# A hybrid encoder layer on one core: attention and memory heads advance on a new step plan, with other counts of convolution taps

## The chip, the cores and the metric

The kernel runs on one core of a Trainium2 chip. The metric is the device time of one execution in microseconds. Five engines work side by side: TensorE (PE in the profile) multiplies, VectorE (DVE), ScalarE (ACT) and GpSimd (POOL) do elementwise work, SyncE (SP) issues DMAs. ScalarE and GpSimd issue DMAs as well.

## The reference, cut to what matters

One layer of a streaming encoder over 512 prompt frames and 64 sample frames (576 tokens, 2048 channels), all in float32.

```
mk, mv = split(mem_prompt @ w_mem_kv)            # 256 memory tokens
ca, cb, cg, q, k, v, ag, mq, mg = split(x @ w_in)
u = ca * sigmoid(cb)                             # conv branch, 1024 channels
y = layer_norm(causal depthwise conv(u, width 31) + conv_b)
conv = silu(y) @ w_pw
att = chunked attention(q, k, v, relative bias)  # 4 heads x 128, own chunk and 8 before it
mem = softmax(mq @ mk^T / sqrt(128)) @ mv        # 4 heads x 128
mix = concat(conv * silu(cg), att * silu(ag), mem * silu(mg))
out = layer_norm(ALPHA * x + mix @ w_out)
```

The outputs are `out` for both groups, the keys and values, the memory keys and values, and the last 30 convolution rows.

## The kernel before

Every float32 operand of a large matmul is split in two parts, `hi` (a cast by ScalarE) and `lo` (the rest, by VectorE), and the product is three matmuls: hi·hi, lo·hi, hi·lo. Weights come as 128x1024 blocks by DMA on SP's queue (`w_load`, line 165), five or more stages ahead, and are split two stages ahead (`w_split`, line 189). A *stage* is what TensorE does with one block.

The stages follow each other in this order on TensorE: the value projection (to about 60 us), 16 column pairs of the input projection by a seven-product scheme (`strassen`, to about 420 us; eight conv pairs, then eight gate pairs), four attention heads (`self_block`: k and q, two stages of 48 matmuls each), the memory projection (`mem_kv`, 16 steps of 18 matmuls), four memory heads (`mem_block`, two stages each), the second half of the output projection (the *out stage* below: 4 column groups n of 4 stages with 28 matmuls), the pointwise convolution product (`tileA(srhs, 1)`), the first half of the output projection, and the closing norm.

Work beside the stages is queued. `pump` (line 210) is called after each stage. It advances the generators in the queue `side` by `steps`, then runs `ntaps` closures of the queue `taps`. A tap is one VectorE instruction of the depthwise convolution over 128x606; each of the eight channel blocks has 31: `first` (which fetches the spilled input `up`), 29 middle ones, and `last`, which makes `y` and spills it. That is 248 in all. The counts are set by `TAP_RATE` (attention), `TAP_RATE_KV` (every second step of `mem_kv`), `TAP_RATE_MEM`, `TAP_RATE_OUT` and `TAPS_OF_PRODUCT` (seven products of a pair).

The generators are `self_attn` (line 692), `mem_attn` (line 588) and `conv_ln` (line 878). Each `yield` ends a step. `self_attn` has seven steps: load bias and cache; scores, maximum, exponential; scaling; transposes of the first two tiles (`pt`, lines 752 to 762); transposes of the rest (lines 771, 775); product with V; gating (`gated`, line 664). A head's generator is queued when its q is done and so runs under the next block's stages; the last head's runs under `mem_kv`, whose six accumulators hold six of the eight PSUM banks. `mem_attn` has five: loads; scores, softmax and scaling; transposes; product; gating. `conv_ln` is queued by the last tap. It takes the mean (one matmul over the sum of the `y`), squares, `var` (line 903), the diagonal `dg` (line 912), the matmuls `ra` that spread it (line 917), eight multiplications and eight SiLUs (lines 923, 924). The eight results are then split to `sx` (lines 1021, 1022) for the pointwise product. `late_mix` pumps until the mix tiles of the coming stage exist, and splits them.

The program is written with a tile framework. It gives every instruction a priority by its place in the program, plans each engine's queue when the program is built, with its own estimates, and lets a later instruction pass where an earlier one's operands or buffers are not expected yet. Tiles of one tag share a fixed number of buffers (`t5` 24, `t6` 11, weights 14, PSUM banks 8).

Of the kernel before, what the change touches and what calls it, by code (L numbers as in the profile page):

```python
# [9 lines left out]
F32 = mybir.dt.float32  # L10
# [5 lines left out]
P = 128  # L16
# [5 lines left out]
H = 4  # L22
# [13 lines left out]
HS = NS_TOK // 2  # L36

C_CA, C_CB, C_CG, C_Q, C_K, C_V, C_AG, C_MQ, C_MG = (0, 1024, 2048, 3072, 3584, 4096, 4608, 5120, 5632)
TAP_RATE = 2
TAP_RATE_KV = 1  # L40
TAP_RATE_MEM = 1
TAP_RATE_OUT = 6
TAPS_OF_PRODUCT = (2, 1, 1, 2, 1, 1, 2)
WARM = 8
CONV_PAIRS = [(C_CA + j * P, C_CB + j * P) for j in range(NCB)]
GATE_PAIRS = [(c + j * P, c + (j + 1) * P) for c, n in ((C_CG, NCB), (C_AG, H), (C_MG, H)) for j in range(0, n, 2)]
# [64 lines left out]
def hymba_kernel(ctx: ExitStack, tc: tile.TileContext, wst, xT, memT, xp, xs, kcT, vc, mkcT, mvc, biasx,  # L111
# [92 lines left out]
                w_load(j)  # L204
        return whi[i], wlo[i]

    side = deque()
    taps = deque()

    def pump(ntaps=0, steps=1):  # L210
        while side and steps:
            try:
                next(side[0])
                steps -= 1
            except StopIteration:
                side.popleft()
        for _ in range(ntaps):
            if not taps:
                break
            taps.popleft()()  # L220

    def drain():
        while side:
            pump()

    sidx = [0]
# [3 lines left out]
        sidx[0] += 1  # L230
        return weights(i)

    def tileA(rhs, nstage, ntaps=0, steps=1):
        accs = [bank("accA") for _ in range(2)]
        klist = list(range(8, 16)) + list(range(8)) if nstage == 2 else list(range(8))
        for s in range(nstage):
            hi, lo = next_stage()
            for kk in range(8):
                ki = 8 * s + kk
                k = klist[ki]  # L240
                ws = slice(kk * P, (kk + 1) * P)
                xh, xl = rhs(k)
                for pi, (mv, stat) in enumerate(((xh, hi), (xl, hi), (xh, lo))):
                    for c, acc in enumerate(accs):
                        nc.tensor.matmul(acc[:, :HALF], stat[:, ws], mv[:, c], start=ki == 0 and pi == 0,  # L245
                                         stop=ki == len(klist) - 1 and pi == 2)
            pump(ntaps, steps)
        return accs

    def tileB(lhs, tiles, sample, klist, ntaps=0, before=None, early=False, steps=1):  # L250
        accs = [bank("accB") for _ in tiles]
        sacc = bank("accS") if sample else None
        nk = len(klist)
        for s in range(nk // 2):
            if before:
                before(s)
            hi, lo = next_stage()
            for kk in range(2):
                ki = 2 * s + kk
                k = klist[ki]  # L260
                ws = slice(kk * 512, (kk + 1) * 512)
                st, en = ki == 0, ki == nk - 1
                if early and st:
                    for t, acc in zip(tiles, accs):
                        nc.tensor.matmul(acc, lhs(k, t)[0], hi[:, ws], start=True, stop=False)
                    for t, acc in zip(tiles, accs):
                        nc.tensor.matmul(acc, lhs(k, t)[0], lo[:, ws], start=False, stop=False)
                    for t, acc in zip(tiles, accs):
                        nc.tensor.matmul(acc, lhs(k, t)[1], hi[:, ws], start=False, stop=False)
                else:  # L270
                    for t, acc in zip(tiles, accs):
                        lh, ll = lhs(k, t)
                        nc.tensor.matmul(acc, lh, hi[:, ws], start=st, stop=False)  # L273
                        nc.tensor.matmul(acc, ll, hi[:, ws], start=False, stop=False)  # L274
                        nc.tensor.matmul(acc, lh, lo[:, ws], start=False, stop=en)  # L275
                if sample:
                    ss = sample(k)
                    nc.tensor.matmul(sacc, ss, hi[:, ws], start=st, stop=False)  # L278
                    nc.tensor.matmul(sacc, ss, lo[:, ws], start=False, stop=en)  # L279
            pump(ntaps, steps)  # L280
        return accs, sacc
# [138 lines left out]
    ysb = [None] * NCB  # L420
    ups = {}
    spilled = set()
    ln_left = [True]
    y_dram = [dram([P, NT], "yd") for _ in range(NCB)]
    s1 = [None]

    def queue_conv(j):
        acc = []
        up = [None]

        def fetch(j):
            ups[j] = t6([P, UPW], "up")
            nc.sync.dma_start(ups[j], up_dram[j])

        def first():
            for i in (j, j + 1):
                if i in spilled and i not in ups:
                    fetch(i)
            up[0] = ups[j]
            a = spool.tile([P, ACCW], F32, tag="t6", bufs=N6, name=nm("acc"))  # L440
            acc.append(a)
            nc.vector.tensor_scalar(a, up[0][:, :ACCW], cw_sb[:, j, 0:1], cp_sb[:, 0, j:j + 1], op0=ALU.mult, op1=ALU.add)

        def tap(t):
            def f():
                nc.vector.scalar_tensor_tensor(acc[0], up[0][:, t:t + ACCW], cw_sb[:, j, t:t + 1], acc[0],  # L446
                                               op0=ALU.mult, op1=ALU.add)
            return f

        def last():  # L450
            t = TAPS - 1
            y = t6([P, NT], "y")
            o = NP_TOK + 30
            for w, o, ys in ((HP, 0, slice(0, HP)), (HS, o, slice(HP, HALF))):
                yv = y.rearrange("p (a b) -> p a b", a=2)[:, :, ys]
                uv, av = (m.rearrange("p (a b) -> p a b", a=2)
                          for m in (up[0][:, o + t:o + t + 2 * w], acc[0][:, o:o + 2 * w]))
                nc.vector.scalar_tensor_tensor(yv, uv, cw_sb[:, j, t:t + 1], av, op0=ALU.mult, op1=ALU.add)
            nc.gpsimd.dma_start(y_dram[j], y)
            if j == 0:  # L460
                s1[0] = y
            elif j == 1:
                y0, s1[0] = s1[0], t6([P, NT], "s1")
                nc.vector.tensor_add(s1[0], y0, y)
            else:
                nc.vector.tensor_add(s1[0], s1[0], y)
            if j == NCB - 1:
                side.append(conv_ln())

        taps.append(first)  # L470
        for t in range(1, TAPS - 1):
            taps.append(tap(t))
        taps.append(last)
# [14 lines left out]
    def conv_sink(j):  # L488
# [5 lines left out]
        def both(c1, sg):  # L494
# [4 lines left out]
            nc.vector.tensor_mul(up[:, 572:636].rearrange("p (a b) -> p a b", a=2), c1[:, :, HP:], sg[:, :, HP:])  # L499
            nc.scalar.copy(cs_sb[:, j, :30], up[:, 512:542])  # L500
            nc.scalar.copy(cs_sb[:, j, 30:], up[:, 606:636])
            nc.gpsimd.dma_start(up_dram[j], up)
            spilled.add(j)
            queue_conv(j)
        return second, both
# [83 lines left out]
    def mem_attn(h, qh, ql, qs):  # L589
# [38 lines left out]
            nc.scalar.activation(pv, pv, AF.Copy, scale=sm[:, t:t + 1])  # L628
        nc.scalar.activation(pss[:64], pss[:64], AF.Copy, scale=sm[:64, 4:5])
        yield  # L630
        pT = []
        for b in range(2):
            tb = bank("mpt")
# [10 lines left out]
            nc.tensor.transpose(tb[:, b * 64:(b + 1) * 64], pss[:64, b * P:(b + 1) * P], ident[:64, :64])  # L644
        sT = t5([P, P], "msT")
        nc.vector.tensor_copy(sT, tb[:, :P])
        yield
        ob = bank("mo")
        os_ = bank("mos")
# [41 lines left out]
    def self_attn(h, qh, ql, qs, kh, kl, k):  # L691
# [54 lines left out]
            nc.scalar.activation(pt[:, po:po + w], pt[:, po:po + w], AF.Copy, scale=sm[:, t:t + 1])  # L746
        nc.scalar.activation(pS[:64, :576], pS[:64, :576], AF.Copy, scale=sm[:64, 4:5])
        yield
        b0 = bank("pt0")
        for t in range(4):  # L750
            pt, po = pplace[t]
# [46 lines left out]
        gated(mix, ob, os_, gate)  # L798
        mixraw[8 + h] = mix

    def self_block(h):
        k = evac2(tileA(xrhs, 2, TAP_RATE, 2), "k")
        nc.gpsimd.dma_start(kT_out[:, h], k.rearrange("p a b -> p (a b)"))
        kh = t5([P, 512], "kh", F32R)
        kl = t5([P, 512], "kl", F32R)
        khv, klv = (m.rearrange("p (a b) -> p a b", a=2) for m in (kh, kl))
        nc.scalar.copy(khv, k[:, :, :HP])
        nc.vector.tensor_sub(klv, k[:, :, :HP], khv.bitcast(F32))
        qh, ql, qs = evac_q(tileA(xrhs, 2, TAP_RATE, 2))
        side.append(self_attn(h, qh, ql, qs, kh, kl, k))  # L810


    mraw = {}
    mv_sb, mk_sb = [], []

    def load_mem(k):
        raw = t5([P, NMEM], "mraw")
        nc.sync.dma_start(raw, memT[:, k])
        mraw[k] = raw

    def mem_kv():
        for k in range(3):
            load_mem(k)
        mkacc = [bank("mkacc") for _ in range(H)]
        mvacc = [bank("mvacc") for _ in range(2)]
        for k in range(KD):
# [38 lines left out]
            mv_sb.append((mvh, mvl))  # L865

    def mem_block(h):
        qh, ql, qs = evac_q(tileA(xrhs, 2, TAP_RATE_MEM, 3))
        side.append(mem_attn(h, qh, ql, qs))


    def bcast_sum(src, name):
# [4 lines left out]

    def conv_ln():
        yield
        for j in range(NCB):  # L880
            ysb[j] = t5([P, NT], "y")
            nc.sync.dma_start(ysb[j], y_dram[j])
# [90 lines left out]
    def out_source(t, acc):  # L973
# [4 lines left out]
        nc.vector.tensor_add(tmp[:NS_TOK], acc[:NS_TOK], tmp[:NS_TOK])  # L978
        return tmp[:NS_TOK]

    for i in range(8, 16):
        if i in mixraw:
            split_mix(i)
# [8 lines left out]

    load_z(0)
    for n in range(4):
        accs, sacc = tileB(mlhs2, range(4), msl, list(range(8, 16)), ntaps=TAP_RATE_OUT, before=late_mix, steps=3)
        if n < 3:
            load_z(n + 1)
        for t, acc in enumerate(accs + [sacc]):
            zt = z[t, n][:P if t < 4 else NS_TOK]
            nc.vector.scalar_tensor_tensor(zt, zt, ALPHA, out_source(t, acc), op0=ALU.mult, op1=ALU.add)  # L1000
# [222 lines left out]
```

## Time and profile before

| | |
|---|---|
| timed runs | 977.73, 981.31, 981.89 us; median 981.31 |
| profiled execution | 984.15 us, span 982.4 us |
| mean granted TensorE clock | 0.98 of full speed |
| PE busy | 949.7 us (97%) |
| DVE, ACT, POOL busy | 713.2, 405.2, 83.7 us |
| moved by DMA | 146 MB, 148 GB/s over the span |

The span runs from the first to the last instruction. Busy time of PE is counted to the modelled end of each matmul, so overlapping matmuls are counted once and a busy PE can still run at half clock: the windows view gives the granted clock of a stretch beside the busy time. The list of waits gives only the time in which an engine had nothing to run, and what ended it.

### The profile page before, as it was taken

How to read it: one execution, taken by the hardware profiler on the slowest of the kernel's cores; microseconds unless marked ns; L12 is line 12 of the kernel's file. 1: busy time of each engine (PE TensorE's matmuls, PEld its weight loads, DVE VectorE, ACT ScalarE, POOL GpSimd, SP SyncE). 2: the span in 40 equal slices, each digit the busy share in tenths (PEclk: the TensorE clock that was granted, in tenths of full speed). 3: DMA queues.
4: the chain of work that ended last, by engine and by line, in shares of the span. 5: the costliest groups of instructions: out<-in, count | busy, mean ns of one | idle time of the engine just before them, and what ended most of it. 6: DMA issues, size and time to landing. Idle time of an engine off the chain costs nothing. (4 is left out here: it accounts for less than half of the span.)

```text
span 982.4 us, 15182 instructions
## 1 busy us (share of the span) xinstructions
PE 949.7 (97%) x6037; PEld 873.4 (89%) x6037; DVE 713.2 (73%) x1002; ACT 405.2 (41%) x691; POOL 83.7 (9%) x144
## 2 busy tenths in 40 slices
PE   8999999999999999998999898999999899999996
PEld 5899999999999999997988787999888789988874
DVE  7864999989979799898244368935697864535576
ACT  6654444454544444434243345346511453421110
POOL 0021111011110000000000000000000000003341
PEclk9999999999999999999899998999999899999997
DMA  9656557566676675653222355424373334232205
GB/s 331 193 165 161 163 155 203 140 170 163 178 205 168 173 200 155 209 168 112 83 105 82 129 191 172 148 99 142 105 245 125 99 113 134 88 107 84 90 7 186
DMA packets 52056, 146.07 MB, mean 149 GB/s; under 512 B 6478, under 2 KB 11086, under 8 KB 51986
## 3 DMA queue, kind: packets, MB, share of 16 engines
q1 hardware_dynamic: 41746, 112.24, 34.5%
q0 software_dynamic: 7648, 27.63, 12.8%
q10 hardware_dynamic: 2592, 5.24, 1.4%
q8 instruction: 47, 0.77, 0.3%
q14 instruction: 23, 0.19, 0.1%
HBM read 125.85 MB, written 19.23 MB: 148 GB/s over the span
## 5 line engine op out<-in xcount | busy, mean ns | idle before, releaser
L196 DVE TENSOR_TENSOR wlo<-wraw,whi 128x1024 fp32r<-128x1024 f32 x183 | 227.0, 1245 | 147.8 <-issue 37.4
L195 ACT CAST whi<-wraw 128x1024 fp32r<-128x1024 f32 x183 | 191.0, 1051 | 266.2 <-DVE wlo L196 151.6
L483 PE MATMUL st<-x,whi 128*128 128x288 f32 x1024 | 205.1, 295 | 3.0 <-ACT neg L549 2.1
L446 DVE SCALAR_TENSOR_TENSOR acc<-up,cw_sb,acc 128x606 f32<-128x606 f32 x232 | 196.6, 847 | 4.0
L483 PEld LDWEIGHTS st<-x,whi 128*128 128x128 f32 x1024 | 163.9, 188 | 4.2 <-ACT neg L549 3.0
L483 PE MATMUL st<-x,wlo 128*128 128x288 f32 x512 | 150.8, 295 | 0.0
L245 PE MATMUL accA<-x,whi 128*128 128x288 f32 x768 | 138.2, 301 | 0.0
L245 PEld LDWEIGHTS accA<-x,whi 128*128 128x128 f32 x768 | 114.5, 191 | 1.8 <-issue 1.2
L483 PEld LDWEIGHTS st<-x,wlo 128*128 128x128 f32 x512 | 96.0, 188 | 0.0
L273 PE MATMUL accB<-whi,mix 128*128 128x512 f32 x224 | 89.3, 399 | 0.0
L275 PE MATMUL accB<-wlo,mix 128*128 128x512 f32 x224 | 88.8, 396 | 0.0
L274 PE MATMUL accB<-whi,mix 128*128 128x512 f32 x224 | 88.4, 395 | 0.0
L245 PE MATMUL accA<-x,wlo 128*128 128x288 f32 x384 | 83.8, 299 | 0.0
L483 PE MATMUL st<-t13h,whi 128*128 128x288 f32 x256 | 75.5, 295 | 0.7 <-ACT pos L544 0.7
L483 PE MATMUL st<-t13h,wlo 128*128 128x288 f32 x256 | 75.5, 295 | 0.0
L483 PE MATMUL st<-t13l,whi 128*128 128x288 f32 x256 | 75.4, 295 | 0.0
L245 PEld LDWEIGHTS accA<-x,wlo 128*128 128x128 f32 x384 | 62.7, 191 | 0.0
L483 PE MATMUL st<-t,whi 128*128 128x288 f32 x256 | 51.4, 295 | 0.0
L275 PEld LDWEIGHTS accB<-wlo,mix 128*128 128x128 f32 x224 | 42.5, 190 | 9.8
L273 PEld LDWEIGHTS accB<-whi,mix 128*128 128x128 f32 x224 | 42.5, 190 | 9.6 <-issue 0.4
L274 PEld LDWEIGHTS accB<-whi,mix 128*128 128x128 f32 x224 | 42.7, 191 | 9.2
L483 PEld LDWEIGHTS st<-t13h,whi 128*128 128x128 f32 x256 | 48.0, 188 | 0.9 <-ACT pos L544 0.9
(329 smaller groups left out, 1590.3 us busy)
## 6 DMA issues: line engine op xcount, KB each, us to landing
wraw<-in_wst_dram SPq DMA_DIRECT2D x151, 512.0 KB, 3.7
wsum<-in_wst_dram POOLq DMA_DIRECT2D x16, 512.0 KB, 9.1
wraw<-in_wst_dram POOLq DMA_DIRECT2D x16, 512.0 KB, 7.6
xraw<-in_xT_dram SPq DMA_DIRECT2D x19, 288.0 KB, 5.6
z<-in_xp_dram SPq DMA_DIRECT2D x16, 256.0 KB, 4.6
out_y_dram<-z SPq DMA_DIRECT2D x16, 256.0 KB, 2.1
upd<-up POOLq DMA_DIRECT2D x8, 318.0 KB, 8.0
up<-upd SPq DMA_DIRECT2D x8, 318.0 KB, 3.7
```

Of the source, the lines that this page charges most:

```text
L195: nc.scalar.copy(hi, src)
L196: nc.vector.tensor_sub(lo, src, hi.bitcast(F32))
L245: nc.tensor.matmul(acc[:, :HALF], stat[:, ws], mv[:, c], start=ki == 0 and pi == 0, stop=ki == len(klist) - 1 and pi == 2)
L273: nc.tensor.matmul(acc, lh, hi[:, ws], start=st, stop=False)
L274: nc.tensor.matmul(acc, ll, hi[:, ws], start=False, stop=False)
L275: nc.tensor.matmul(acc, lh, lo[:, ws], start=False, stop=en)
L446: nc.vector.scalar_tensor_tensor(acc[0], up[0][:, t:t + ACCW], cw_sb[:, j, t:t + 1], acc[0], op0=ALU.mult, op1=ALU.add)
L483: nc.tensor.matmul(acc[:, :HALF], stat[:, ws], mv, start=first and k == 0 and i == 0, stop=k == 7 and i == 2, skip_group_check=not first)
```

## The change

- The single queue `side` becomes four: `self`, `mem0`, `mem1` (memory heads by parity) and `norm`. A pump advances each of the first three by two steps and `norm` by one.
- `self_attn` gets one bare `yield` after the scaling: eight steps, four pumps of two. `mem_attn` gets two after the scaling and one after the transposes: eight steps.
- The first three memory tiles are asked for between k and q of the last attention head.
- The spill of `up` is issued by ScalarE, that of `y` later: at the fifth tap of the next block, or in `conv_ln`.
- Tap counts: see the first hunk.
- Ahead of the out stage the last memory head is advanced by two steps.

```diff
-TAP_RATE = 2
+TAP_RATE = 4
 TAP_RATE_KV = 1
-TAP_RATE_MEM = 1
-TAP_RATE_OUT = 6
-TAPS_OF_PRODUCT = (2, 1, 1, 2, 1, 1, 2)
+TAP_RATE_MEM = 2
+TAP_RATE_OUT = 5
+TAPS_OF_PRODUCT = (1, 2, 1, 1, 1, 1, 1)
...
-    side = deque()
+    sides = {q: deque() for q in ("self", "mem0", "mem1", "norm")}
     taps = deque()
 
-    def pump(ntaps=0, steps=1):
+    def advance(q, steps):
+        side = sides[q]
         while side and steps:
             try:
                 next(side[0])
                 steps -= 1
             except StopIteration:
                 side.popleft()
+
+    def pump(ntaps=0, steps=2):
+        for q in sides:
+            advance(q, 1 if q == "norm" else steps)
         for _ in range(ntaps):
...
         def tap(t):
             def f():
+                if t == 4 and spill:
+                    spill.pop()()
...
-            nc.gpsimd.dma_start(y_dram[j], y)
+            spill.append(lambda: nc.gpsimd.dma_start(y_dram[j], y))
...
-            nc.gpsimd.dma_start(up_dram[j], up)
+            nc.scalar.dma_start(up_dram[j], up)
...
             nc.scalar.activation(pv, pv, AF.Copy, scale=sm[:, t:t + 1])
         nc.scalar.activation(pss[:64], pss[:64], AF.Copy, scale=sm[:64, 4:5])
         yield
+        yield
+        yield
         pT = []
...
         nc.vector.tensor_copy(sT, tb[:, :P])
+        yield
         yield
         ob = bank("mo")
...
         nc.scalar.activation(pS[:64, :576], pS[:64, :576], AF.Copy, scale=sm[:64, 4:5])
         yield
+        yield
         b0 = bank("pt0")
...
-        qh, ql, qs = evac_q(tileA(xrhs, 2, TAP_RATE, 2))
-        side.append(self_attn(h, qh, ql, qs, kh, kl, k))
+        if h == H - 1:
+            for m in range(3):
+                load_mem(m)
+        qh, ql, qs = evac_q(tileA(xrhs, 2, TAP_RATE))
+        sides["self"].append(self_attn(h, qh, ql, qs, kh, kl, k))
...
     def mem_kv():
-        for k in range(3):
-            load_mem(k)
...
-        qh, ql, qs = evac_q(tileA(xrhs, 2, TAP_RATE_MEM, 3))
-        side.append(mem_attn(h, qh, ql, qs))
+        qh, ql, qs = evac_q(tileA(xrhs, 2, TAP_RATE_MEM))
+        sides[f"mem{h % 2}"].append(mem_attn(h, qh, ql, qs))
...
     def conv_ln():
         yield
+        spill.pop()()
...
+    advance("mem1", 2)
     for i in range(8, 16):
...
-        accs, sacc = tileB(mlhs2, range(4), msl, list(range(8, 16)), ntaps=TAP_RATE_OUT, before=late_mix, steps=3)
+        accs, sacc = tileB(mlhs2, range(4), msl, list(range(8, 16)), ntaps=TAP_RATE_OUT, before=late_mix)
```

## Rows read from the trace of the kernel before

**Rows 1.** The page's busy time of each engine, share of the span, instructions
```profile
PE 949.7 (97%) x6037; PEld 873.4 (89%) x6037; DVE 713.2 (73%) x1002; ACT 405.2 (41%) x691; POOL 83.7 (9%) x144
```

**Rows 2.** TensorE's waits, whole span: for whom, total us, times, longest
```profile
PE mvacc L837 <- ACT mh L831: 5.0, 2, 4.6
PE pt L752 <- issue: 3.9, 1, 3.9
PE pt L752 <- ACT pA L746: 2.5, 2, 1.3
PE ra L917 <- DVE dg L912: 2.5, 1, 2.5
PE st L483 <- ACT neg L549: 2.1, 1, 2.1
PE pt L771 <- DVE pL L756: 1.2, 1, 1.2
...
PE pt L775 <- DVE pL L766: 1.0, 1, 1.0
```

**Rows 3.** Windows, TensorE alone: us, PE busy (matmuls), clock, DMA share, GB/s
```profile
455.68:462.05 6.37, 6.37 (x50) 1.00 0.13 51
467.99:476.48 8.49, 8.49 (x51) 0.74 0.10 37
...
562.96:568.17 5.21, 5.21 (x19) 0.51 0.61 196
568.17:570.97 2.80, 2.80 (x20) 1.00 0.47 136
591.80:596.77 4.97, 2.29 (x17) 0.86 0.67 201
596.77:602.06 5.29, 5.29 (x18) 0.50 0.01 3
780.18:782.78 2.60, 2.60 (x11) 0.50 0.03 6
...
797.49:803.94 6.45, 6.45 (x30) 1.00 0.24 81
```

**Rows 4.** Windows, all engines: PE, PEld, DVE, ACT, POOL busy, clock, DMA
```profile
421.50:480.54 59.04, 55.13 (x384) 53.28 (x383) 44.95 (x67) 21.68 (x39) 1.40 (x4) 0.94 0.36 124
480.54:516.15 35.61, 34.28 (x247) 32.39 (x246) 14.39 (x27) 13.16 (x29) 0.68 (x2) 1.00 0.28 100
...
780.18:786.35 6.17, 6.17 (x18) 5.06 (x19) 5.55 (x11) 3.97 (x6) 0.00 (x0) 0.50 0.01 3
```

**Rows 5.** Timeline, TensorE: start, us, instruction, idle time before it
```profile
504.45 0.33 PE L752 MATMUL pt<-ident,pA 128*128 128x128 f32 x1 [1.26 <-ACT pA L746]
```

**Rows 6.** Timeline, VectorE: gating of the first attention head
```profile
481.00 0.69 DVE L664 TENSOR_TENSOR mixa<-so,gate 128x512 f32<-128x512 f32 x1 [2.77 <-DMA gate<-gated]
```

**Rows 7.** Taps: the page's group, and the first tap in VectorE's timeline
```profile
L446 DVE SCALAR_TENSOR_TENSOR acc<-up,cw_sb,acc 128x606 f32<-128x606 f32 x232 | 196.6, 847 | 4.0
...
100.32 0.60 DVE L442 TENSOR_SCALAR acc<-up,cw_sb,cp_sb 128x606 f32<-128x606 f32 x1 [7.50 <-DMA up<-upd]
```

**Rows 8.** Timeline, SP's queue at the start of the memory projection
```profile
558.42 0.33 SPq L157 DMA_DIRECT2D wraw<-in_wst_dram  x1
558.80 0.42 SPq L818 DMA_DIRECT2D mraw<-in_memT_dram  x1
```

**Rows 9.** Timeline, VectorE at the last head's transposes
```profile
591.78 1.73 DVE L446 SCALAR_TENSOR_TENSOR acc<-up,cw_sb,acc 128x606 f32<-128x606 f32 x2
593.42 0.68 DVE L756 TENSOR_TENSOR pL<-pt,pT 128x512 fp32r<-128x512 f32 x1
```

**Rows 10.** Timeline, ScalarE in the conv norm
```profile
784.67 1.28 ACT L924 ACT_TABLE_LOAD   x1
785.96 6.19 ACT L924 ACTIVATE y<-y,cp_sb 128x576 f32<-128x576 f32 x8
...
793.29 0.67 ACT L1021 CAST sx<-y 128x576 fp32r<-128x576 f32 x1
```

More of the change, by code (lines that the diff above doesn't have):

```diff
@@ L222, in drain @@
     def drain():
-        while side:
+        while any(sides.values()):
             pump()
@@ L231, in next_stage, with tileA @@
         return weights(i)
-    def tileA(rhs, nstage, ntaps=0, steps=1):
+    def tileA(rhs, nstage, ntaps=0, steps=2):
         accs = [bank("accA") for _ in range(2)]
@@ L248, in tileA, with tileB @@
         return accs
-    def tileB(lhs, tiles, sample, klist, ntaps=0, before=None, early=False, steps=1):
+    def tileB(lhs, tiles, sample, klist, ntaps=0, before=None, early=False, steps=2):
         accs = [bank("accB") for _ in tiles]
@@ L422, in hymba_kernel @@
     spilled = set()
+    spill = []
     ln_left = [True]
@@ L467, in last @@
             if j == NCB - 1:
-                side.append(conv_ln())
+                sides["norm"].append(conv_ln())
         taps.append(first)
@@ L799, in self_attn, with load_mem @@
         mixraw[8 + h] = mix
+    mraw = {}
+    mv_sb, mk_sb = [], []
+    def load_mem(k):
+        raw = t5([P, NMEM], "mraw")
+        nc.sync.dma_start(raw, memT[:, k])
+        mraw[k] = raw
     def self_block(h):
-        k = evac2(tileA(xrhs, 2, TAP_RATE, 2), "k")
+        k = evac2(tileA(xrhs, 2, TAP_RATE), "k")
         nc.gpsimd.dma_start(kT_out[:, h], k.rearrange("p a b -> p (a b)"))
@@ L808, in self_block @@
         nc.vector.tensor_sub(klv, k[:, :, :HP], khv.bitcast(F32))
-        qh, ql, qs = evac_q(tileA(xrhs, 2, TAP_RATE, 2))
-        side.append(self_attn(h, qh, ql, qs, kh, kl, k))
[L813 to L819, printed above, removed]
+        if h == H - 1:
[3 more added lines that the diff above has]
+        sides["self"].append(self_attn(h, qh, ql, qs, kh, kl, k))
     def mem_kv():
-        for k in range(3):
-            load_mem(k)
         mkacc = [bank("mkacc") for _ in range(H)]
```

## The prediction

> **What bounds the kernel now.** I read the page's busy times first, then TensorE's list of waits, then the windows that show its clock, and last the timeline around each wait.
>
> TensorE is busy 949.7 of 982.4 us; no other engine comes near [rows 1]. Where it runs at full speed nothing but fewer matmuls would help, and the change removes none. So the question is the 33 us in which it stood idle, and the time at the lower clock behind each idle stretch. The list of waits [rows 2] names them: 3.9 and 2.5 us before the transposes of the attention heads (L752), 5.0 before the memory projection (L837), 1.2 and 1.0 before further transposes (L771, L775), 2.5 before the `ra` matmuls of the conv norm (L917), 2.1 in the first conv pair (L483). The list has no line for the memory heads (L602 to L656) and none for the out stage other than `ra`.
>
> The windows [rows 3] price the clock. A stage of 48 projection matmuls takes 6.37 us; the one after the first head's wait takes 8.49 at 0.74. A step of the memory projection takes 2.80 us; the one after its first wait takes 5.21 at 0.51, the one after the transposes of the last head 5.29 at 0.50. After the `ra` wait 6.17 us run at 0.50 [rows 4]. In the block from 480.54 us, which holds a transpose wait of 1.26 us [rows 5], the clock is 1.00 [rows 4]. So the waits of the first head, of the projection, of the last head's transposes and of `ra` are each followed by 2 to 3 us of loss, the one of 1.26 by none.
>
> **The change, part by part.** Sums are in the profiled execution's own time, 984.15 us (span 982.4); the median of the three timed runs, 981.31, lies 2.84 lower, and I carry the difference over.
>
> *Attention heads.* Before, the softmax's scaling and the first transposes are two steps of one pump, so TensorE meets the transposes before ScalarE has scaled: the third and fourth step both follow the second stage. Now a bare yield stands between. With two steps a stage the eight steps are: loads and scores after stage 1, scaling after 2, all transposes after 3, product with V and gating after 4. The transposes come one stage (6.37 us) later, and the longest wait was 3.9 [rows 2]. Saved for the first head: 3.9 idle and 8.49 - 6.37 = 2.1 behind it: 6.0. For heads 1 and 2: the 2.5 of [rows 2] (two times). Late next is the gating: its DVE instruction waited 2.77 us for a gate loaded a stage ahead of it [rows 6]; now it is in the same pump as the product, and behind it on DVE stand four taps and the evacuation of q. The scores that need that q come after the product and one more stage of 6.37 us. From the product's end DVE needs 0.69 for the gating, 3.4 for four taps and an evacuation shorter than a tap: 4.9, or 7.7 with the gate 2.77 late again. So 0, at worst 1.3 at each of three heads; I take 0.
>
> *Taps.* The 248 DVE operations of the convolution are the same; only their places move. Counting pumps: the conv pairs take 119 (before 148), attention 64 (32), the memory projection 8 (8), memory heads 16 (8), and the out stage gets 41 at 5 a stage (52 at 6). Both leave the last tap in the out stage's ninth pump. In attention a head now carries 16 taps of 847 ns [rows 7], 13.6 us, on top of 14.39 us of DVE in its block, whose 27 instructions hold no tap [rows 4]: 28 of some 34 us. It fits, at 81%. In the conv pairs DVE gets lighter, and TensorE waits there for 2.1 us, before the first tap exists. Cost 0, between -0.9 and the rival below.
>
> *Spills.* The first tap waited 7.50 us for its spilled input [rows 7]. A quicker landing starts the taps earlier, but TensorE doesn't wait for them. ScalarE already waits for the same DVE products in two copies just before, so the issue there adds no wait. Cost 0. The late issue of the `y` spill frees GpSimd's queue from a wait; nothing on TensorE hangs on it: 0.
>
> *Memory tiles asked for sooner.* The first `mraw` was issued at 558.80, right behind a weight load that had stood until a stage ended [rows 8], and the projection began 4.6 us after the last matmul (the longest of the 5.0). Three tiles issued a whole head half earlier (two stages, 12.7 us) are there. Saved: 4.6, and 5.21 - 2.80 = 2.4 behind it: 7.0.
>
> *The last head inside the memory projection.* From 591.80 to 596.77 TensorE was busy for 2.29 us [rows 3]; the transposes' casts stood in DVE's queue behind two taps [rows 9], while six of eight banks were held by the projection. Idle 2.7, and 5.29 - 2.80 = 2.5 behind it: 5.2 in all. Now the head runs through in pumps 1 to 4 rather than 1 to 7, two steps at a time, with the same two free banks and the same DVE load. No row shows the new order. Bounds: all 5.2 saved, or nothing saved and the stall paid once more. The nearest row is the stall itself, so I take half: 2.6.
>
> *Memory heads.* They show no wait now, so there is nothing to save. The last head's product and gating now come after the out stage's third stage, and the fourth needs its split. Behind the product stand 14 matmuls (3.2 us) that don't need it; against them stand the gating, 0.69 [rows 6], a cast of 0.67 (that of the same shape in [rows 10]), a subtraction of like size, and a gate that can be 2.77 late. Between 0 and 2.8; I take 1.0, since the planner, which lets a later instruction pass where an earlier one isn't ready, has left no wait in this stretch so far.
>
> *Conv norm.* Before, it advanced three steps a pump: `var`, the scaling diagonals and `ra` met in one. Now it takes one step a pump, queued after stage 9: the mean after 11, `var` after 14, `ra` after 15, the rest after 16. Saved: 2.5 idle and half of the 6.17 at half clock, 3.1: 5.6. But the pointwise stage follows stage 16. In the trace the first operand (`sx`) is cast 13.1 us after `ra` starts [rows 10]: 2.60 of `ra` itself, a table load of 1.28, eight SiLUs in 6.19, and 3.0 of copies and weight casts between. At full clock `ra` is 1.3 shorter, and half of the 3.0 may stand elsewhere: 10.3 to 11.8, then 0.67 for the cast. Stage 16 ends 1.3 + 6.45 = 7.8 after `ra` starts [rows 3]. The new wait is 3.2 to 4.7; I take 3.9, plus 2.4 behind it (the 2.1 to 3.1 of the other waits): +6.3. If this cover held, it would cost 0; at the worst 7.8.
>
> The Trainium skill's page "ScalarE: Activation LUTs", section "What ACT_TABLE_LOAD costs", gives a switch of tables about 1.28 us and a drain of 1.38 besides. The trace agrees with the first figure (1.28) and not with the second: the SiLUs start at 785.96, as the load ends [rows 10]. By that rule the new wait would be an estimated 1.4 longer and the sum 1.4 smaller; the row decides.
>
> Sum: -6.0 - 2.5 - 7.0 - 2.6 + 1.0 - 5.6 + 6.3 = **-16.4**. That is 967.8 in the profiled execution's time and **964.9** against the median.
>
> **Rivals.** *A, the new wait before the pointwise stage doesn't come* (the norm's DVE and ScalarE work is packed closer than in the trace), or the last head's stall goes altogether: -22.7 or -19.0, both -25.3: 956 to 962, say 957. For it: nothing else is queued on ScalarE then. Against: eight SiLUs alone fill a stage.
>
> *B, the memory projection takes it back*: the last head stalls as before or twice (+2.6 to +7.8), since DVE is busy there and the banks are two: 968 to 973, say 971. For it: the stall of [rows 9] came from queue order alone.
>
> *C, slower: DVE in the attention stretch.* Four taps stand in DVE's in-order queue between an attention step and the evacuation that TensorE's banks and scores wait for. DVE is idle for 21.2 of the 35.6 us in the block now; most of that is waiting in line for TensorE, ScalarE or a gate. If half of the 16 taps a head fall outside those holes, that is 6.8 us a head, 27 over four: 992. It decides from 4.1 us a head (five taps). Against: nothing waits for taps, and between 421 and 480 DVE did 44.95 busy us with only the waits already told [rows 4].
>
> *D, the change doesn't do what it says*: the planner sets each queue by its own estimates, so the steps end up in the old places and only the memory tiles come sooner, with the new norm wait against it: -7.0 + 6.3 + 1.0, about 981.
>
> **How the numbers follow.** Forecast 0.52 (own range 960 to 970), A 0.20, B 0.15, C 0.05, D 0.08. The range takes the forecast with A and B and their bounds: all savings and no new wait give -26.3, 955, less 2 for what is left unpriced (transposes that ran at half clock, the lighter DVE of the conv pairs); the worst of norm, gate and a repeated stall give -16.4 + 1.5 + 1.8 + 7.8 = -5.3, 976. So 953 to 976. A difference under 0.5% (4.9 us) can't be told from none here: faster means under 976.4. Faster 0.52 + 0.20 + 0.15 + 0.01 = 0.88; same 0.07 (most of D); slower 0.05 (C).
>
> **What would show it.** In the changed profile the list of waits should have no line of more than 0.5 us at the heads' first transposes and none of 4 us at the first memory matmul, with clock 1.00 in both places; `ra` should follow a full stage with no wait; and a new wait of 3 to 5 us should stand before the first `sx` matmul, released by ScalarE's cast, with half clock behind it. DVE should show taps all through the attention stretch. Wrong would be: waits of DVE or ScalarE spread over the attention stages (C), no wait before `sx` (A), or the same transposes waiting (D).

## The result and the profile after

The changed kernel takes **970.28 us** (median of four runs, 968.01 to 972.11), the kernel before 981.5 beside it (977.73 to 981.89): ratio 0.9893, 95% interval 0.986 to 0.9926, so 7 to 14 us faster. Forecast were 964.9, with a range of 953 to 976. Direction and range held; the gain was 11 us and not 16. The profiled execution took 969.66 (span 967.7), 14.5 less than that of before.

The page's busy line of the changed kernel answers to [rows 1]:

```profile
PE 942.2 (97%) x6037; PEld 867.5 (90%) x6037; DVE 713.2 (74%) x1002; ACT 404.1 (42%) x691; POOL 79.3 (8%) x136
```

The same 6037 matmuls. Now TensorE's waits, as in [rows 2] (for whom, total us, times, longest):

```profile
PE accA L251 <- ACT sx L1037: 3.4, 1, 3.4
PE msc L616 <- DMA mkc<-in_mkcT_dram: 1.8, 1, 1.8
PE pt L788 <- DVE pL L779: 1.7, 1, 1.7
PE pt L784 <- DVE pL L769: 1.1, 1, 1.1
PE msc L613 <- DVE ql L692: 0.9, 1, 0.9
```

Gone are the first transposes (3.9 and 2.5), the first memory matmul (4.6 of the 5.0) and `ra` (2.5). The forecast wait before `sx` (L1037) has come, with 3.4. Not forecast is the memory heads' scores (L613, L616), which waited for nothing before. And the last head's transposes (L784, L788), in which half of the loss was to go, still wait 1.1 and 1.7 (and 0.4 at the product behind, L801).

Windows of the changed kernel, TensorE alone (columns as in [rows 3]): the first step of the memory projection; the second half of the last memory head's scores; what follows them; a stretch of 6.45 us with `ra` in it (from 782.54); the start of the pointwise product.

```profile
545.84:548.74 2.90, 2.73 (x16) 1.00 0.88 292
671.05:676.05 5.00, 2.30 (x11) 0.89 0.56 184
676.05:679.30 3.25, 3.25 (x11) 0.64 0.02 5
780.72:787.17 6.45, 6.45 (x33) 1.00 0.29 81
794.01:797.01 3.00, 3.00 (x13) 0.57 0.88 341
797.01:800.01 3.00, 3.00 (x22) 0.86 0.02 5
```

And with all engines (as in [rows 4]): the whole attention stretch, the same time of the span as the block of [rows 4] (the heads stand elsewhere in it now), and the stretch of the last head's transposes.

```profile
412.26:542.80 130.54, 130.54 (x956) 126.27 (x955) 103.96 (x166) 53.37 (x110) 3.90 (x10) 1.00 0.40 133
480.54:516.15 35.61, 35.61 (x261) 34.16 (x260) 30.86 (x50) 13.19 (x29) 1.23 (x3) 1.00 0.34 118
570.84:575.84 5.00, 3.49 (x9) 2.71 (x10) 4.29 (x9) 1.93 (x4) 0.00 (x0) 0.67 0.27 93
```

TensorE is busy all 130.54 us of the attention, at full clock, with VectorE busy for 80%: rival C is out. The last head's transposes are followed by a clock of 0.67, the scores by 0.64, the first `sx` matmuls by 0.57.

Why the scores waited stands in SP's queue of the changed kernel:

```profile
660.50 0.43 SPq L595 DMA_DIRECT2D gate<-gated  x1
670.92 0.33 SPq L157 DMA_DIRECT2D wraw<-in_wst_dram  x1
671.29 0.43 SPq L600 DMA_DIRECT2D mkc<-in_mkcT_dram  x1
```

and TensorE meets them so (timeline, idle time before in brackets):

```profile
672.01 0.38 PE L613 MATMUL msc<-mkw,ql 128*128 128x256 f32 x1 [0.88 <-DVE ql L692]
...
675.04 1.09 PE L616 MATMUL msc<-mkc,qs 128*64 128x256 f32 x2 [1.82 <-DMA mkc<-in_mkcT_dram]
```

The queue stood from 660.5 to 670.92 behind a weight load, whose buffer VectorE's split `wlo` gave free only then, as it did at the start of the memory projection in [rows 8]. The head's key cache was asked for behind it, and landed 3.7 us after its issue.

The conv norm on ScalarE, as in [rows 10]:

```profile
785.30 1.28 ACT L939 ACT_TABLE_LOAD   x1
786.60 6.18 ACT L939 ACTIVATE y<-y,cp_sb 128x576 f32<-128x576 f32 x8
792.80 0.58 ACT L992 COPY ztmp<-accS 64x512 f32<-64x512 f32 x1
793.29 4.68 ACT L1037 CAST sx<-y 128x576 fp32r<-128x576 f32 x8
```

Stage 16 had ended at 790.6; eight SiLUs and a copy of that stage's result stand ahead of the first `sx`. The SiLUs start 0.02 us behind the table load. So this trace too lacks the drain of 1.38 us that the Trainium skill's page "ScalarE: Activation LUTs", section "What ACT_TABLE_LOAD costs", adds.

### The profile page after: what moved, and what is told of

It is laid out like the page before. It is cut to its first block, busy times and chain, and to the rows that moved or that the text cites. A ratio compares the mean times of both kernels' runs of the same rounds, so it can differ in the third digit from the quotient of the medians.

```text
span 967.7 us, 15182 instructions
## 1 busy us (share of the span) xinstructions
PE 942.2 (97%) x6037; PEld 867.5 (90%) x6037; DVE 713.2 (74%) x1002; ACT 404.1 (42%) x691; POOL 79.3 (8%) x136
## 5 line engine op out<-in xcount | busy, mean ns | idle before, releaser
L251 PE MATMUL accA<-x,whi 128*128 128x288 f32 x768 | 134.6, 297 | 0.0
L251 PE MATMUL accA<-sx,whi 128*128 128x288 f32 x256 | 45.8, 302 | 3.4 <-ACT sx L1037 3.4
```

## The experiments

Each ratio is to the kernel before on the same chip, with its 95% interval; that kernel's medians were 980.74 beside the first four; 982.07 beside the old memory heads, the caches sooner, the one step a pump and the best version; 979.47 beside the other four. Versions timed on different chips are compared by their ratios; where the intervals of two overlap, the times alone don't show a difference, and the traces carry the argument. "The changed kernel" stands at 0.9893, and at 0.990 in a second timing (below).

### The memory tiles alone, on the kernel before

```diff
+        if h == H - 1:
+            for m in range(3): load_mem(m)
         qh, ql, qs = evac_q(tileA(xrhs, 2, TAP_RATE, 2))
...
-        for k in range(3): load_mem(k)      # in mem_kv
```

> The kernel before with one edit alone: the first three memory tiles are asked for between k and q of the last attention head. Theory (the first memory matmul waited for its tile, which stood behind a weight load in SP's queue): the 4.6 us wait before the first mvacc matmul and the 2.4 us of half clock behind it go, -7.0 us against the kernel before, about 974.5; the waits at the attention heads' transposes stay at 3.9 and 2.5. Rival (the wait only moves to the cast of the tile or to the banks, or the stretch gives it back at the last head's transposes): -0 to -3 us, and a wait of 2 us or more somewhere in the memory projection that was not there.

979.32 us, ratio 0.9989 [0.9965, 1.0012]. **The 7 us are not the tiles' alone.** TensorE's waits:

```profile
PE pt L752 <- issue: 3.8, 1, 3.8
PE mvacc L838 <- ACT mh L832: 3.2, 2, 2.7
PE pt L752 <- ACT pA L746: 2.5, 2, 1.3
```

The tiles were asked for at 535.5, yet the first matmul still waits 2.7 of the 4.6 us. ScalarE's timeline shows behind what:

```profile
554.56 0.65 ACT L679 CAST qh<-accA 128x256 fp32r<-128x256 f32 x2 [8.10 <-PE accA L245]
555.74 1.04 ACT L195 CAST whi<-wraw 128x1024 fp32r<-128x1024 f32 x1 [0.54 <-DVE wlo L196]
556.69 0.27 ACT L681 COPY qs<-accA 128x32 f32<-128x32 f32 x2
556.85 1.03 ACT L832 CAST mh<-mraw 128x256 fp32r<-128x256 f32 x3
```

The cast `mh` is queued behind the evacuation of the last q, which itself waits for TensorE to finish q. With the tile there, the evacuation is late next. The half clock behind the wait is gone in this trace (window, TensorE alone; 5.21 us at 0.51 in [rows 3]):

```profile
557.32:560.30 2.98, 2.98 (x19) 1.00 0.89 288
```

So this execution has some 4 of the 7 us. But at 975.5 us it is the fastest of twelve; the median says 1.4, and the interval bounds the saving at 3.4.

### The bare yield in the attention heads alone, on the kernel before

```diff
         nc.scalar.activation(pS[:64, :576], pS[:64, :576], AF.Copy, scale=sm[:64, 4:5])
         yield
+        yield
```

> The kernel before with one edit alone: the bare yield after the attention head's scaling, so that the transposes come one stage later. Theory (TensorE met the transposes before ScalarE had scaled): the 3.9 and 2.5 us waits at the first transposes go, with some 2 to 3 us of half clock behind the first: -8.5 to -11 us, about 971 to 973. Rival (the gain of the change in this stretch comes from the other places of the taps): waits remain at the transposes or reappear at the product, -0 to -4 us.

**963.86 us**, ratio 0.983 [0.9798, 0.9862]: one line does more than the whole change, and more than was expected of it (971 to 973). The profiled execution is 20.9 us shorter than that of before: 13.9 in the attention (3.0 of them only moved out of it) and 4.2 in the memory projection; the other 2.8 lie in stretches without attention heads. What is left of the waits named in [rows 2]:

```profile
PE ra L918 <- DVE dg L913: 2.5, 1, 2.5
...
PE pt L772 <- DVE pL L757: 2.0, 1, 2.0
PE mvacc L838 <- ACT mh L832: 1.5, 1, 1.5
```

The transposes wait no more, and the wait at the memory projection is down to 1.5 without any tile asked for sooner. TensorE's timeline of this kernel shows what stands there now:

```profile
542.53 0.43 PE L245 MATMUL accA<-x,wlo 128*128 128x288 f32 x2
542.80 0.39 PE L789 MATMUL so<-pT,vw 128*128 128x512 f32 x1
...
545.64 0.43 PE L795 MATMUL sos<-pTS,vs 64*128 64x64 f32 x2
547.57 0.50 PE L838 MATMUL mvacc<-whi,mh 128*128 128x512 f32 x1 [1.50 <-ACT mh L832]
```

With eight steps the product with V of the third head runs after the last q, 542.8 to about 546: 3 us of work that have to be done anyway, now in the place of the stall, while tile and cast arrive. The first step behind ran at full clock (2.90 us, against 5.21 in [rows 3]).

### The conv norm alone, on the kernel before

```diff
+    normq = deque()       # advanced by one step at each pump
...
-                side.append(conv_ln())
+                normq.append(conv_ln())
```

> The kernel before with one edit alone: the conv norm has its own queue and takes one step a pump. Theory (the step rate moves the wait from ra to the pointwise stage): the 2.5 us wait at ra is gone, a wait of 3 to 4 us stands before the first sx matmul, and the time is within 2 us of the kernel before. Rival A of the prediction (the cover holds): no wait before sx, -5.6 us.

982.93 us, ratio 1.0012 [0.999, 1.0035]: nothing. The wait of `ra` is gone, and in its place the list has

```profile
PE accA L252 <- ACT sx L1028: 3.4, 1, 3.4
```

### The changed kernel with the norm started a pump sooner

```diff
     def conv_ln():
-        yield
         spill.pop()()
```

> The changed kernel with the conv norm's first bare yield taken out, so that every step of the norm comes one out stage sooner. Theory (the norm ends one stage too late for the pointwise product): the 3.4 us wait before the first sx matmul and some 2 us of half clock behind it go, ra still has a stage to itself: about -5.4 us against the changed kernel's 970.3, so 965, ratio to before about 0.9835. Rival (the spilled y, or the squares, are not there a stage sooner, so the wait shows up at the mean or at var): no gain, 970, with a wait at the mean, var or ra matmuls.

966.72 us, ratio 0.985 [0.9816, 0.9884]: by the ratios some 4 less than the changed kernel, though the two intervals overlap. `ra` still has no wait, and that before `sx` has shrunk to

```profile
PE accA L251 <- DVE sx L1037: 0.5, 1, 0.5
```

and the 3 us behind it run at 1.00. So the 3.4 us and the half clock behind them are a matter of one pump.

### The changed kernel with the memory heads as before

```diff
-        yield
-        yield        # the two bare ones after the scaling
...
-        yield        # the bare one after the transposes
...
-        qh, ql, qs = evac_q(tileA(xrhs, 2, TAP_RATE_MEM))
-        sides[f"mem{h % 2}"].append(mem_attn(h, qh, ql, qs))
+        qh, ql, qs = evac_q(tileA(xrhs, 2, TAP_RATE_MEM, 3))
+        sides["mem0"].append(mem_attn(h, qh, ql, qs))
...
-    advance("mem1", 2)
...
-        accs, sacc = tileB(mlhs2, range(4), msl, list(range(8, 16)), ntaps=TAP_RATE_OUT, before=late_mix)
+        accs, sacc = tileB(mlhs2, range(4), msl, list(range(8, 16)), ntaps=TAP_RATE_OUT, before=late_mix, steps=3)
```

> The changed kernel with the memory heads alone as before: one queue, five steps, three steps a pump, no advance ahead of the out stage. Theory: the changed kernel loses about 4.5 us at the third memory head (scores that wait 0.9 us for ql and 1.8 us for the head's key cache, and about 2 us at half clock behind), because the new step plan lets TensorE reach them sooner and the cache's load stands in SyncE's queue behind a weight load. Without it: 965 to 967 us, no wait at the memory scores, the memory heads' stretch back from 69.6 to about 67.4 us. Rival: the loss in that stretch comes from the tap count (2 instead of 1 a stage), which stays here: then 969 to 971 us and the waits remain.

966.68 us, ratio 0.9837 [0.9811, 0.9864]. No wait at the memory scores. From the first matmul of the memory heads' first q to the first `sx` matmul TensorE needs 183.3 us here (67.36 to the out stage, 115.96 from there), in the changed kernel 187.6 (69.60 and 117.96). The price of the memory heads' new plan is 4.2 us: 2.7 of waits, the rest clock. The tap count, which stayed, is no part of it.

### The last memory head's caches asked for sooner

```diff
+        cache = load_cache(h) if h == H - 1 else None
         qh, ql, qs = evac_q(tileA(xrhs, 2, TAP_RATE_MEM))
...      # and mem_attn takes the cache that it is given
```

> The changed kernel with the key and value caches of the last memory head asked for before its q stages instead of after. Theory: the cache stood in SyncE's queue behind a weight load; asked earlier it is there, the wait of 1.8 us at the memory scores goes, and with it the half clock behind: 966 to 968 us; the wait for ql (0.9) may stay. Rival: the load is not what decides, another operand (ql, qs or a bank) takes its place and the time stays at 969 to 971 us.

968.4 us, ratio 0.9849 [0.9821, 0.9878], 0.4 above what was expected, and with an interval that overlaps that of the changed kernel. The loads go out at 655.90, ahead of the weight load that holds the queue; the wait for `mkc` is gone, that of 0.9 for `ql` stays. Behind it alone the clock stays up (windows of the scores and of what follows):

```profile
671.40:675.43 4.03, 3.15 (x21) 1.00 0.38 121
675.43:678.68 3.25, 3.25 (x15) 1.00 0.17 57
```

From the first memory q to the first `sx` matmul this trace needs 184.2 us, 3.4 less than the changed kernel's: one load and the clock behind it make up most of the 4.2.

### The last attention head one step a pump

```diff
             if k % 2:
-                pump(TAP_RATE_KV)
+                pump(TAP_RATE_KV, 1)
```

> The changed kernel with one step a pump in the memory projection instead of two, so that the last attention head spreads over eight pumps there. Theory 1 (the stall of 1.1 and 1.7 us comes from four pumps packed too close, with the casts pL not yet made when TensorE comes to the transposes): the waits fall under 1 us in all and the time by 3 to 5 us, to 965 to 967. Theory 2 (it comes from the two free banks and from taps ahead of the casts in VectorE's queue, whatever the pace): the waits stay near 2.8 us and the time within 1.5 us of the changed kernel's.

966.17 us, ratio 0.9831 [0.9805, 0.9857]: the time of the first theory. The profiled execution, 970.97, is the slowest of seven. The waits in it agree with neither: the three of 1.1, 1.7 and 0.4 became a single one of 2.0. The memory projection takes 58.49 us instead of 60.62. So the two steps a pump, which the prediction counted as a saving, cost the changed kernel 2 us and more.

### The changed kernel once more, and without taps in the memory projection

> The changed kernel once more, beside the three others of this set, so that differences of a few microseconds can be read from one chip: 968 to 972 us, as before.

970.44 us, ratio 0.990 [0.9875, 0.9924].

```diff
-TAP_RATE_KV = 1
-TAP_RATE_MEM = 2
+TAP_RATE_KV = 0
+TAP_RATE_MEM = 3
```

> The changed kernel with no convolution taps in the memory projection and three instead of two at each stage of the memory heads, so that the norm is queued where it was. Theory: the last attention head's transposes wait 1.1 and 1.7 us because taps stand in VectorE's queue ahead of the casts pL; without taps there the two waits fall under 1 us together and the half clock behind them goes: 3 to 4.5 us less than the changed kernel. Rival: the two free banks decide (a bank is free again only when VectorE and ScalarE have read it, taps or none); the waits stay within 0.5 us of 2.8 and the time within 1.5 us.

969.55 us, ratio 0.989 [0.9866, 0.9913], 0.9 less by the medians; the waits are

```profile
PE pt L788 <- DVE pL L779: 1.3, 1, 1.3
...
PE pt L784 <- DVE pL L769: 1.0, 1, 1.0
```

**My theory fell**: with every tap out of the way the two waits lose 0.5 us together. One part of it came in the profiled execution: the clock behind the waits stayed at 1.00 (0.77 and then 0.89 in that of the changed kernel beside it), and the memory projection took 58.55 us instead of 60.65. The medians don't show a gain of that size. In the changed kernel VectorE's timeline does show a cast behind taps, as [rows 9] did:

```profile
567.07 1.73 DVE L455 SCALAR_TENSOR_TENSOR acc<-up,cw_sb,acc 128x606 f32<-128x606 f32 x2
568.72 0.69 DVE L769 TENSOR_TENSOR pL<-pt,pT 128x512 fp32r<-128x512 f32 x1
```

but without them VectorE stands idle ahead of the same cast:

```profile
570.58 0.69 DVE L769 TENSOR_TENSOR pL<-pt,pT 128x512 fp32r<-128x512 f32 x1 [2.12 <-ACT pT L768]
571.53 1.22 DVE L196 TENSOR_TENSOR wlo<-wraw,whi 128x1024 fp32r<-128x1024 f32 x1 [0.25 <-ACT whi L195]
572.67 0.68 DVE L779 TENSOR_TENSOR pL<-pt,pT 128x512 fp32r<-128x512 f32 x1
```

A `pL` needs ScalarE's `pT`, and that needs the transposes; weight splits stand between on both engines. This fits the rival (two banks, each free only when both engines have read it). That the banks decide was not tried by itself.

### The old taps and spills in the changed kernel

```diff
-TAP_RATE = 4         # and 2, 5 and (1, 2, 1, 1, 1, 1, 1) for memory heads, out stage, products
+TAP_RATE = 2         # and 1, 6 and (2, 1, 1, 2, 1, 1, 2)
...
-            nc.scalar.dma_start(up_dram[j], up)
+            nc.gpsimd.dma_start(up_dram[j], up)
-            spill.append(lambda: nc.gpsimd.dma_start(y_dram[j], y))
+            nc.gpsimd.dma_start(y_dram[j], y)
...      # and the later spills of y go
```

> The changed kernel with the tap counts of before, the spill of up issued by GpSimd and that of y at once. The prediction put both edits at nothing: within 2 us of the changed kernel, with the attention block at 130.5 us as there. Rival: two taps a stage leave VectorE freer in the attention and ahead of the last head (a gain), or the taps missing there end later, so that the norm is queued later and the wait before the first sx grows (a loss of 3 us or more).

968.94 us, ratio 0.9883 [0.9858, 0.9909], against 970.44 beside it: the difference of 1.5 lies inside the intervals. The attention takes 130.54 us in both. Taps and spills bring nothing that can be measured.

### The best version

The kernel before with three parts: the yield, the tiles sooner, and the norm in its own queue without `conv_ln`'s first bare yield.

> The kernel before with three parts alone: the bare yield in the attention heads, the memory tiles asked for sooner, and the conv norm in a queue of its own, one step a pump, started one pump sooner than in the change. Theory: the yield alone gave 963.9; the tiles take away the 1.5 us that the first matmul of the memory projection still waits, and the norm the 2.5 us before ra with its half clock, with 0.5 left before the first sx: together 3 to 5 us less, 959 to 961 us. Rival: the norm started sooner costs elsewhere as much as it saves (the out stage 114.9 against 116.5 us, but the last part 172.9 against 172.0) and the tiles give nothing: 963 to 965 us.

**960.49 us**, ratio 0.977 [0.9742, 0.9797], as expected. Its waits include

```profile
PE pt L779 <- DVE pL L764: 2.0, 1, 2.0
...
PE accA L252 <- DVE sx L1030: 0.5, 1, 0.5
```

and none at the first memory matmul over 0.2, none at `ra`, none in the memory heads. The tiles, worth nothing measurable by themselves, leave no wait once the product covers what was late behind them.

Then the same with the memory projection's taps moved to the memory heads:

```diff
-TAP_RATE_KV = 1
-TAP_RATE_MEM = 1
+TAP_RATE_KV = 0
+TAP_RATE_MEM = 2
```

> The best version so far (yield, tiles sooner, norm in its own queue one pump sooner: 960.5) with no taps in the memory projection and two instead of one at each stage of the memory heads. Theory: the wait of 2.0 us at the last head's transposes, which follows taps in VectorE's queue, goes: 958 to 959.5 us, the memory projection 55 us instead of 57.0. Rival: the wait stays or moves to another transpose and the time stays at 960 to 961.5.

962.55 us, ratio 0.9824 [0.9796, 0.9852]: no better than the best version, by the medians 2 worse and by the ratios 5; neither theory nor rival allowed for that. The memory projection gains 0.6 (56.39 us), its wait falls to 1.5, and the memory heads lose 5.9 (73.27). VectorE's timeline there:

```profile
648.29 3.51 DVE L453 SCALAR_TENSOR_TENSOR acc<-up,cw_sb,acc 128x606 f32<-128x606 f32 x4
651.88 0.69 DVE L647 TENSOR_TENSOR mpl<-mpt,mph 128x512 fp32r<-128x512 f32 x1
```

Four taps ahead of the first `mpl`, a weight split ahead of the second: TensorE stood idle 1.4 us in this stage (0.2 and 0.9 of it for the two) and ran the next 6.37 us at 0.53. This is rival C's mechanism, at a place where TensorE's product (651.90) follows the transposes (649.89) after 2 us. In the best version no tap runs on VectorE from 620 to 680, and nothing waits there.

## Why the prediction was right, and where it was off

By stretches of TensorE's records (profiled executions, before to after), the steps measured as follows; an idle time belongs to the stretch it ends.

| step | forecast | measured | from |
|---|---|---|---|
| three attention heads | -8.5 | -10.9 | attention 144.43 to 130.54; 3.03 of it is the product that moved out |
| first memory step | -7.0 | -6.9 | wait and first step, 4.58 + 5.21 to 2.90 |
| last attention head | -2.6 | +0.7 | the other 15 steps, 57.03 to 57.72 |
| memory heads | +1.0 | +4.2 | 183.33 to 187.56, against the changed kernel with the old memory heads |
| conv norm | +0.7 | -0.1 | 185.17 to 183.33 from the first memory q to the first `sx` (the latter with the old memory heads); 172.00 to 173.72 from there |
| taps, spills | 0 | -1.7 | all that stands ahead of the attention, 413.96 to 412.26 |
| sum | -16.4 | -14.7 | difference of the spans |

That the sum came so near is in part luck: the attention gave 2.4 more than forecast and chance 1.7, the last head and the memory heads together took 6.5 more, and the first memory step reached its size by another cause.

**Attention heads: right, mechanism and place.** No wait at the first transposes, clock 1.00. Before, idle 6.4 us and a clock loss of 4.5 went together; I had priced 2.1 of that loss and named 2 as unpriced.

**First memory step: right size, wrong cause.** The step that failed reads "Three tiles issued a whole head half earlier (two stages, 12.7 us) are there. Saved: 4.6, and 5.21 - 2.80 = 2.4 behind it: 7.0." Alone they bring 1.4 us by the medians, inside the interval of no change; in the trace they remove 1.9 of the 4.6 and the half clock. The yield alone removes 3.1 of the 4.6 and the half clock, because it moves a product into the gap. I had listed which operand came last in [rows 8], but not what would be late next (`mh` behind q's evacuation), nor that the heads' new steps put other work in front of this wait. In the changed kernel tiles and yield overlap, so the sum came out.

**Last attention head: failed.** "I take half": of 2.6 us nothing was saved. Two steps a pump press the same chain into four pumps; one step a pump leaves one wait instead of three, and 966.17 us. With the yield alone, which keeps the one step, the other 15 steps fall from 57.03 to 55.16. I had read [rows 9] as a queue behind taps; without the taps the waits are nearly the same. That is rival B (971 us): its mechanism came, at its low end.

**Memory heads: failed by 3.2.** I looked at the end (product, gating, split, gate) and found no reason for a wait; there is none there. It came at the beginning. The two steps taken ahead of the out stage are the last head's loads and its scores. Before, these scores stood at about 700 us (their last matmul with `mkw` began at 700.5), behind the first out stage (from 692.58); now they begin at 670.4, behind q and the third head's product, where `ql` is not made and the cache not there. I had priced the head's end, not the DMAs of its first step (`mkc`, `mvc`), and the queue they enter is the one that [rows 8] show standing behind a weight load.

**Conv norm: right, both terms.** 3.4 of wait (forecast 3.9) and 1.7 of lost clock (2.4), against a saving of 5.4 (forecast 5.6): the stretch up to the first `sx` matmul is 1.8 shorter (185.17 less 183.33), although that matmul now starts 3.8 us behind the start of stage 16's last one, before 0.2. Alone on the kernel before it changes nothing (1.0012). Rival A, no such wait, did not come, but needs only one pump: 0.5 us when the norm starts sooner.

**Taps and spills: right.** Their -1.7 is chance: over all profiled executions these stretches took 352.4 to 355.6 us, with old counts and new alike.

**Rivals C and D** failed: no wait in the attention, and the steps are where the program put them.

From sum to median: with the sizes above but without the chance in the conv stretches, the sum is -13.0. The medians say -11.2, with an interval that holds both. I had carried the whole sum over from a profiled execution of 984.15, longer than any of the three timed runs. Later runs of that kernel went from 975.7 to 987.6. A long one holds clock losses that others do not have, and a change can't save those in all runs.

So of the change's parts one line (the yield) brings 17 us by the medians (980.74 to 963.86); the others give 6 back.

## What to carry to other kernels

When a stall is followed back to its last operand, look at what is late next, and at which work could stand in its place: moving a product of 3 us into the gap took away more of the wait (3.1 us of 4.6) than asking earlier for the operand (1.9), and only both together left none. When steps are advanced, the DMAs that they issue need their lead as well, and an in-order queue in front of them can hold back a small load behind a large one that waits for its buffer. Try the parts of a change alone: here one line beat the whole, and three of the parts, one of them retimed by a pump, beat both.

## What the runs showed of the hardware

The clock does not fall after every stall of a given length. At the last head's transposes two kernels have the same wait, 2.0 us for `pL`, and much the same busy time before it. With the one step a pump in the changed kernel, TensorE's clock fell (windows, all engines):

```profile
577.44:582.44 5.00, 3.67 (x26) 3.16 (x25) 4.96 (x7) 3.05 (x4) 0.00 (x0) 1.00 0.53 170
582.44:587.44 5.00, 4.36 (x20) 3.43 (x21) 4.59 (x9) 2.91 (x7) 0.00 (x0) 0.74 0.34 122
587.44:592.44 5.00, 5.00 (x30) 4.58 (x30) 3.83 (x6) 1.66 (x3) 0.00 (x0) 0.92 0.47 163
```

In the best version it did not (its second window is as busy, but with 27 matmuls instead of 20):

```profile
576.90:581.90 5.00, 3.70 (x27) 3.19 (x25) 4.96 (x7) 3.08 (x4) 0.00 (x0) 1.00 0.61 160
581.90:586.90 5.00, 4.34 (x27) 3.51 (x28) 4.94 (x11) 2.91 (x7) 0.00 (x0) 1.00 0.40 139
586.90:591.90 5.00, 5.00 (x34) 4.53 (x34) 5.00 (x8) 2.41 (x4) 0.00 (x0) 1.00 0.75 232
```

The prediction put 2 to 3 us of lost clock behind each wait that had shown it. That is a size with a chance: of the waits here that of 0.9 was followed by none, 2.0 by some or none, 2.7 (the tiles alone) by none, 3.4 by 1.7 us. What tips it in the case of 2.0 stays open.
